# Feed-forward block of a hybrid decoder: 13 of 16 pairs of the upper projection by Strassen's scheme, lower projection by two tiles

## The chip, the cores and the metric

The kernel runs on one core of one Trainium2 chip, in one launch. The metric is the device time of that launch in microseconds (us); lower is better. The program is one long stream of instructions for five engines: TensorE (PE: matmuls and, as PEld, its weight loads), VectorE (DVE), ScalarE (ACT), GpSimd (POOL) and SyncE (SP), which here issues the DMAs. Each engine works through its own queue in order and waits at semaphores for the others.

## The reference

The reference is one inference step of a decoder layer for 512 prompt tokens and 64 sample tokens, 576 in all. After a state-space branch, an attention branch and their merge comes the part that matters here, for a residual `h` of width 1024:

```
u2 = rmsnorm(h, norm2_w)
h = h + jnp.square(jax.nn.relu(u2 @ w_up)) @ w_down     # w_up 1024x4096, w_down 4096x1024
```

and a last rmsnorm gives the outputs `y_prompt` and `y_sample`. All arrays are 32-bit floats.

## The kernel before, in words

**Precision.** TensorE reads 32-bit operands as `fp32r`, a rounded form. So each operand is kept as two tiles: `hi`, a rounded copy made by ScalarE (L122), and `lo`, the remainder raw - hi made by VectorE (L123). A product is then three matmuls, hi\*hi, hi\*lo and lo\*hi, into the same PSUM bank (`mm3`, L138 to L145). `weights` (L125 to L132) loads one 512 KB tile of weights (128 partitions x 1024) into a raw tile `wr`, of which there are two, and splits it.

**Upper projection** (L1203 to L1235). The 4096 columns of `w_up` are 32 tiles f of 128 columns. For each f and each of two halves of 288 tokens, `up` runs 8 x 3 = 24 matmuls of 128x288 (weights stationary, the tokens `u2h`, `u2l` moving) into a bank of kind `a` (three banks). ScalarE takes the relu out of the bank (L1207), VectorE squares it (L1208), ScalarE rounds it to `hh` (L1209), VectorE makes the remainder `hl` (L1211). The first three tiles are done first over 256 and then over 320 tokens (`PARTS`), so that they can start before the last tokens are normalised.

**Lower projection** (`add_product`, L1171 to L1186). Now the activations are stationary: for one of five blocks of 128 rows (four of prompt tokens; block 4 carries the hi and lo of the sample tokens side by side) and one half of the 1024 output columns, the matmuls of 128x512 over some tiles k of the inner dimension add into a bank of kind `s` (three banks). VectorE then adds that bank to the residual `h2` (L1186). Before, a group is four tiles f: 12 matmuls a bank (8 in block 4), 112 matmuls and 10 additions a group, 8 groups. The weights of a group, four row tiles of `w_down`, are split into `dh` and `dl` (seven buffers each).

**Order.** The groups are software-pipelined by hand: `ups(s + 1)` stands ahead of the lower projection of group s (L1238 to L1245). A scheduler then lays the instructions of every engine out in a fixed order, from a model of their times, before the program runs; on the chip each engine follows that order, whatever the real times are. Buffers of a tag are reused in turn, so an instruction that writes a tile can wait for the last reader of the tile that had the buffer before.

**Around it.** L1188 to L1197 are the output projection `w_out` and the second rmsnorm (`norm2`, `turn2`), which fill `u2h` and `u2l`. `final` and `last` normalise and store the result. POOL has almost nothing to do in this part.

Of the kernel before, what the change touches and what calls it, by code (L numbers as in the profile page):

```python
# [70 lines left out]
def body(ctx, tc, a, o):  # L71
# [12 lines left out]
    def pst(tag):  # L84
        return psp.tile([128, 512], FT, tag=tag, name=tag, bufs=PSB[tag])
# [22 lines left out]
    def flat(t):  # L108
        return t.rearrange("p a b -> p (a b)")
# [40 lines left out]
    def rows(src, n):  # L150
        return bass.AP(tensor=src.tensor, offset=src.offset, ap=[[0, 128], [1, n]])
# [938 lines left out]
    for t in ORDER:  # L1090
        load_x(t, h2[:, t, :])
    pool.memset(h2[64:128, 4, :], 0.0)

    p4w = ctx.enter_context(tc.tile_pool(name="p4w", bufs=1, reuse_waits="tile", side="right"))

    def row_weights(src, r0, n, at=(p4w, ("dl", "dh"), 7)):

        return [[flat(x) for x in weights([(flat, src[r0 + 128 * k:r0 + 128 * k + 128, :])], at)] for k in range(n)]

    wo = row_weights(a["w_out"][0], 0, 4)  # L1100
    def norm_rows(name):
        row = p4.tile([128, D], FT, tag="wrow", name="wrow", bufs=1)
        sy.dma_start(row, rows(a[name], D))
        return row
# [64 lines left out]
    PIECES = ((0, 512), (512, 768), (768, 1024))  # L1169

    def add_product(t, xh, xl, ws, cuts=((0, 512), (512, 1024)), banks="s"):  # L1171

        tok = slice(128 * t, 128 * t + 128)
        for c0, c1 in cuts:
            cc = slice(c0, c1)
            nb[0] += 1
            ps = pst(banks[nb[0] % len(banks)])[:, :c1 - c0]
            for k, (wh, wl) in enumerate(ws):
                if t < 4:
                    terms = (xh[k][:, tok], wh), (xl[k][:, tok], wh), (xh[k][:, tok], wl)  # L1180
                else:
                    terms = (xh[k][:, tok], wh), (xh[k][:, tok], wl)
                for i, (x, w) in enumerate(terms):
                    pe.matmul(ps, x, w[:, cc], start=(k == 0 and i == 0),  # L1184
                              stop=(k == len(ws) - 1 and i == len(terms) - 1))
            dve.tensor_tensor(h2[:, t, cc], h2[:, t, cc], ps, op=OP.add)  # L1186

    wrow = norm_rows("norm2_w")  # L1188
    turns = []
    for q in range(2):  # L1190
        ws = row_weights(a["w_out"][0], 512, 4) if q else wo
        for t in ORDER:
            add_product(t, [mgh[:, 4 * q + k, :] for k in range(4)], [mgl[:, 4 * q + k, :] for k in range(4)], ws, banks="sa")
            if q == 1:
                turns.append(norm2(t))
                if t in (0, 1, 2):
                    turns.pop(0)()  # L1197
    frow = norm_rows("final_norm_w")
    p4a_stack.close()

    p5 = ctx.enter_context(tc.tile_pool(name="p5", bufs=1, reuse_waits="tile"))

    def up(w, f, hh, hl, c0, c1):  # L1203
        ps = pst("a")
        mm3(ps, w, u2h, u2l, c0, c1)
        r = p5.tile([128, 320], FT, tag="r", name="r", bufs=3)[:, :c1 - c0]
        act.activation(r, ps[:, :c1 - c0], AF.Relu)  # L1207
        dve.tensor_tensor(r, r, r, op=OP.mult)  # L1208
        act.activation(hh[f][:, c0:c1], r, AF.Copy)  # L1209
        for dst, e0, e1 in rest(hh[f], hl[f], c0, c1):  # L1210
            dve.tensor_tensor(dst, r[:, e0 - c0:e1 - c0], hh[f][:, e0:e1].bitcast(FT), op=OP.subtract)  # L1211

    def ups(s, ws=None):
        hh = [p5.tile([128, NQ + NS], FR, tag="hh", name="hh", bufs=9) for _ in range(4)]
        hl = [p5.tile([128, NP], FR, tag="hl", name="hl", bufs=9) for _ in range(4)]

        def w_up(f):
            return whole(a["w_up"][0], 0, 512 * s + 128 * f)

        f0 = 0  # L1220
        if s == 0:
            f0 = 3
            w3 = [w_up(f) for f in range(3)]
            for c in PARTS:
                for f in range(3):
                    up(w3[f], f, hh, hl, *c)
                    if turns:
                        turns.pop(0)()
        for f in range(f0, 4):
            w = w_up(f)  # L1230
            for c in HALVES:
                up(w, f, hh, hl, *c)
            if ws is not None:
                ws += row_weights(a["w_down"][0], 512 * (s - 1) + 128 * f, 1)
        return hh, hl  # L1235

    prev = ups(0)
    for s in range(8):  # L1238
        ws = [] if s < 7 else row_weights(a["w_down"][0], 512 * s, 4)
        nxt = ups(s + 1, ws) if s < 7 else None  # L1240
        for i, t in enumerate(ORDER):
            add_product(t, *prev, ws, **({"cuts": PIECES} if s == 7 and i == 4 else {}))
            if s == 7 and i > 0:
                final(ORDER[i - 1])
        prev = nxt  # L1245
# [26 lines left out]
```

## Time and profile before

| what | value |
|---|---|
| three runs | 1486.2 us median (1485.6 to 1489.74) |
| profiled execution | 1491.02 us, span 1489.2 us |
| PE busy over the span | 1440.7 us (97%) |
| DVE busy | 975.5 us (66%) |
| ACT busy | 693.8 us (47%) |
| POOL busy | 327.7 us (22%) |
| granted TensorE clock, mean | 0.991 |

Times in the rows are us from the start of the span unless marked ns. A line such as `L145` is that of the kernel above. "busy" of a stretch is the time in which the engine had at least one instruction running; `x` counts instructions. `out<-in` gives the tiles that an instruction writes and reads; buffer numbers are left out. The span is the time between the first and the last instruction; 1.8 us of the profiled execution lie outside.

### The profile page before, as it was taken

Reading aid. Unit: us, or ns where it says so; the run is one execution under the profiler, and the core shown is the slowest. Engines: PE = TensorE matmul, PEld = TensorE weight load, DVE = VectorE, ACT = ScalarE, POOL = GpSimd, SP = SyncE. Lnnn points to the kernel's source line nnn. Section 1 sums busy time; section 2 is a strip of 40 time slices with the busy share of each in tenths; the row PEclk is TensorE's granted clock in tenths of the full one; section 3 lists DMA queues with packets and bytes.
Section 4 is the critical chain, followed back from the end, with each engine's and each line's share of the span. In section 5 each row is a group of like instructions: output and inputs, shape, how many; then the busy total and the mean of one; then the engine's idle time right before and its main releaser. Section 6 shows DMA issues by size and latency. Waiting matters only on the chain.

```text
span 1489.2 us, 26558 instructions
## 1 busy us (share of the span) xinstructions
PE 1440.7 (97%) x9964; PEld 1293.0 (87%) x9964; DVE 975.5 (66%) x2011; ACT 693.8 (47%) x1546; POOL 327.7 (22%) x479
## 2 busy tenths in 40 slices
PE   7899999999999998999999999999999999999998
PEld 6898989988887887889688888898898898899886
DVE  6699989988868667582555777665654453444435
ACT  5454365546656654443655777732352232232211
POOL 1100010426546335342323632100100000000001
PEclk9999999999999999999999999999999999999999
DMA  7324465777888877878975522146152322231202
GB/s 185 100 57 124 120 195 155 209 216 217 249 252 204 248 219 205 245 193 258 304 216 160 147 81 83 39 147 192 34 150 77 100 89 59 81 112 58 87 27 71
DMA packets 276379, 222.08 MB, mean 149 GB/s; under 512 B 39741, under 2 KB 239281, under 8 KB 276226
## 3 DMA queue, kind: packets, MB, share of 16 engines
q1 hardware_dynamic: 271002, 201.50, 47.6%
q0 software_dynamic: 5248, 18.88, 3.7%
q8 instruction: 79, 1.29, 0.4%
q14 instruction: 50, 0.41, 0.1%
HBM read 175.50 MB, written 44.07 MB: 147 GB/s over the span
## 4 chain that ended last, share of the span: by engine, by line
PE 81%; DMA 8%; DVE 5%; ACT 2%; SPq 2%; POOL 1%; issue 1%; POOLq 0%; DVEq 0%; ACTq 0%
PE w L145 25%; PE s L1184 16%; PE a L145 14%; PE w L1046 7%; PE s L1012 2%; PE a L1184 2%; PE s L878 2%; PE s L741 1%; DMA xt<-d_x 1%; PE a L1002 1%; DMA bc<-d_ac 1%; PE a L901 1%; PE s L753 1%; PE s L870 1%; DVE wl L123 1%
## 5 line engine op out<-in xcount | busy, mean ns | idle before, releaser
L145 PE MATMUL w<-uh,wh 128*128 128x288 f32 (+1 forms) x1168 | 358.4, 307 | 8.8 <-ACT tg L284 2.2
L145 PE MATMUL w<-uh,wl 128*128 128x288 f32 (+1 forms) x1168 | 354.8, 304 | 0.0
L145 PE MATMUL w<-ul,wh 128*128 128x288 f32 (+1 forms) x1168 | 352.2, 302 | 0.0
L145 PEld LDWEIGHTS w<-uh,wh 128*128 128x128 f32 x1168 | 223.4, 191 | 15.8 <-issue 3.4
L123 DVE TENSOR_TENSOR wl<-wr,wh 128x1024 fp32r<-128x1024 f32 x129 | 164.2, 1273 | 110.0 <-ACT wh L122 99.6
L145 PEld LDWEIGHTS w<-ul,wh 128*128 128x128 f32 x1168 | 223.3, 191 | 2.9 <-issue 2.2
L145 PEld LDWEIGHTS w<-uh,wl 128*128 128x128 f32 x1168 | 222.1, 190 | 1.5 <-issue 0.7
L122 ACT ACTIVATE wh<-wr 128x1024 fp32r<-128x1024 f32 x129 | 136.4, 1057 | 146.0 <-PE w L145 91.7
L145 PE MATMUL a<-u2h,wh 128*128 128x288 f32 (+2 forms) x512 | 151.4, 296 | 0.0
L145 PE MATMUL a<-u2l,wh 128*128 128x288 f32 (+2 forms) x512 | 151.2, 295 | 0.0
L145 PE MATMUL a<-u2h,wl 128*128 128x288 f32 (+2 forms) x512 | 151.2, 295 | 0.0
L122 ACT ACTIVATE dh<-wr 128x1024 fp32r<-128x1024 f32 x40 | 42.5, 1063 | 182.9 <-PE s L1184 138.3
L1186 DVE TENSOR_TENSOR h<-h,s 128x512 f32<-128x512 f32 (+1 forms) x91 | 61.1, 679 | 100.9 <-PE s L1184 100.9
L1184 PE MATMUL s<-dl,hh 128*128 128x512 f32 (+1 forms) x324 | 126.9, 392 | 0.0
L1184 PE MATMUL s<-dh,hh 128*128 128x512 f32 (+1 forms) x324 | 126.8, 392 | 0.0
L155 POOL TENSOR_TENSOR rs<-rs,cst 128x1 f32<-128x1 f32 (+2 forms) x15 | 8.3, 552 | 441.4 <-DVE rs L154 441.3
L1184 PE MATMUL s<-dh,hl 128*128 128x512 f32 (+1 forms) x260 | 101.7, 391 | 0.0
L145 PEld LDWEIGHTS a<-u2l,wh 128*128 128x128 f32 x512 | 96.1, 188 | 0.6
L145 PEld LDWEIGHTS a<-u2h,wh 128*128 128x128 f32 x512 | 96.1, 188 | 0.6
L145 PEld LDWEIGHTS a<-u2h,wl 128*128 128x128 f32 x512 | 96.1, 188 | 0.0
L123 DVE TENSOR_TENSOR dl<-wr,dh 128x1024 fp32r<-128x1024 f32 x40 | 49.0, 1225 | 49.9 <-ACT dh L122 49.8
L1046 PE MATMUL w<-ysh,wh 128*128 128x288 f32 x256 | 78.4, 308 | 0.2 <-DVE ms L1051 0.2
(390 smaller groups left out, 3220.2 us busy)
## 6 DMA issues: line engine op xcount, KB each, us to landing
wr<-in_w_in_dram SPq DMA_DIRECT2D x64, 512.0 KB
wr<-in_w_up_dram SPq DMA_DIRECT2D x32, 512.0 KB
wr<-in_w_down_dram SPq DMA_DIRECT2D x32, 512.0 KB
st<-in_state_ssm_dram SPq DMA_DIRECT2D x16, 512.0 KB
bc<-d_ac SPq DMA_DIRECT2D x32, 256.0 KB
out_dram<-st SPq DMA_DIRECT2D x16, 512.0 KB
wr<-in_w_ssm_proj_dram SPq DMA_DIRECT2D x16, 512.0 KB
EB<-d_ec SPq DMA_DIRECT2D x40, 128.0 KB
```

The costliest lines, as they stand in the source:

```text
L122: act.activation(hi, raw, AF.Copy)
L123: (lo_eng or dve).tensor_tensor(lo, raw, hi.bitcast(FT), op=OP.subtract)
L145: pe.matmul(ps[:, :c1 - c0], p[:, k, :], x[:, c0:c1], start=(k == 0 and i == 0), stop=(k == 7 and i == 2))
L741: pe.matmul(py[64 * (hh % 2):64 * (hh % 2) + 64, 128 * (hh // 2):128 * (hh // 2) + n], xt[:n, 64 * hh:64 * hh + 64], mt, start=True, stop= ...
L753: pe.matmul(pi[:, 128 * i:128 * i + 128], G.hT[:, 128 * i:128 * i + 128], CT[:, c0:c0 + n], start=True, stop=True)
L870: pe.transpose(pv[:, i, :], Kg[q][:, 256 * i + 128 * hp:256 * i + 128 * hp + 128], idf)
L878: pe.matmul(v[64 * hp:64 * hp + 64], QZ[:, hp, :], kk, start=True, stop=True)
L901: pe.matmul(py[h, 0:128], PTs[:, s, h], Vg[s // 4][:, 256 * (s % 4) + 128 * hp:256 * (s % 4) + 128 * hp + 128], start=(s == 0), stop=False)
L1012: pe.matmul(py[64 * e:64 * e + 64, 0:256], Vt[:, j, kv:kv + 64], PT[:, e, j], start=(j == 0), stop=False)
L1046: pe.matmul(ps[:, :HQ], p[:, k, mc], x[k][:, c0:c1], start=(k == 0 and i == 0), stop=(k == 3 and i == 2))
L1184: pe.matmul(ps, x, w[:, cc], start=(k == 0 and i == 0), stop=(k == len(ws) - 1 and i == len(terms) - 1))
L1186: dve.tensor_tensor(h2[:, t, cc], h2[:, t, cc], ps, op=OP.add)
```

## The change

The 32 column tiles of `w_up` are taken as 16 pairs. Six tiles (three pairs) are computed as before. The other 13 pairs are computed by a scheme of the Strassen-Winograd kind: the pair's 1024x256 weights are four blocks of 512x128 (a11, a12 in the raw tile `left`, a21, a22 in `right`; the inner dimension is cut in two, and the two tiles f are the other index), the tokens are four blocks of 512x288. Seven block products of 4 x 3 = 12 matmuls take the place of eight. The sums of weights are made in place in the raw tiles by VectorE (four subtractions or additions of 128x512 a pair), and the four forms that arise are split: `fa` and `fb` into the usual buffers `wh`/`wl` (three of each), `fc` into `gh`/`gl` and `fd` into `eh`/`el`, of which there is one each. The raw tiles of every other pair come from a second pair of buffers, `wr2`. The sums of token blocks are made once, in `token_sums`; one of them overwrites a block of `u2h`, `u2l`. Products are combined on VectorE (`plus`, seven a pair, one operand in PSUM), then squared. The squaring moves from VectorE to ScalarE. Halves of tokens are laid out as 256 prompt tokens and 32 sample tokens each.

The lower projection runs by groups of two tiles f in place of four (14 groups, and one of four at the end), with four buffers each for `dh`, `dl` in a new pool that takes the place of the pool of `w_out`; the latter has six buffers in place of seven.

```diff
-    def row_weights(src, r0, n, at=(p4w, ("dl", "dh"), 7)):
+    WO = (p4w, ("dl", "dh"), 6)
+    wo = row_weights(a["w_out"][0], 0, 4, WO)
...
+    def squared(src, x, h, r=None):
+        hh, hl = x
+        r = small("r", 3) if r is None else r
+        act.activation(r, src, AF.Relu)
+        act.activation(r, r, AF.Square)
+        p, q = slice(256 * h, 256 * h + 256), slice(NP + 32 * h, NP + 32 * h + 32)
+        act.activation(hh[:, p], r[:, 0:256], AF.Copy)
+        act.activation(hh[:, q], r[:, 256:HQ], AF.Copy)
+        dve.tensor_tensor(hl[:, p], r[:, 0:256], hh[:, p].bitcast(FT), op=OP.subtract)
+        dve.tensor_tensor(hh[:, NQ + 32 * h:NQ + 32 * h + 32], r[:, 256:HQ], hh[:, q].bitcast(FT), op=OP.subtract)
...
+    def token_sums():
+        E = (dve, dve, dve, dve)
+        for k in (0, 2):
+            def B(i, j):
+                return [u[:, 4 * i + k:4 * i + k + 2, HQ * j:HQ * j + HQ].bitcast(FT) for u in (u2h, u2l)]
+            v, w = [flat(q5.tile([128, 8, 128], FT, tag="wr2", name="tr", bufs=2))[:, 0:2 * HQ].rearrange("p (k c) -> p k c", k=2)
+                    for _ in range(2)]
...
+            diff(v, b12, b11, E[0])
+            done(th[:, 0, k:k + 2], tl[:, 0, k:k + 2], v)
+            less(v, b22, v, E[2])
+            done(th[:, 1, k:k + 2], tl[:, 1, k:k + 2], v)
+            less(w, b21, v, E[3])
+            done(th[:, 2, k:k + 2], tl[:, 2, k:k + 2], w)
+            diff(v, b22, b12, E[1])
+            done(u2h[:, k:k + 2, HQ:NQ], u2l[:, k:k + 2, HQ:NQ], v)
+
+    tags = ["a", "w", "a", "a", "w"]
+
+    def quick_pair(f):
+        hh = act_tiles(2)
+        at = (q5, "wr2") if f % 4 else (wp, "wr")
+        left, right = [at[0].tile([128, 8, 128], FT, tag=at[1], name=at[1], bufs=2) for _ in range(2)]
+        for i, x in enumerate((left, right)):
+            sy.dma_start(x, block(w_up, 0, 128 * f + 128 * i))
+        a11, a12, a21, a22 = left[:, 0:4], left[:, 4:8], right[:, 0:4], right[:, 4:8]
...
+        fa = two(wp, ("wh", "wl"), WB[1])
+        split(left, *fa)
+        fd = two(p5, ("eh", "el"), 1, 4)
+        split(a22, *fd)
+        dve.tensor_tensor(a22, a21, a22, op=OP.add)
+        dve.tensor_tensor(a21, a11, a21, op=OP.subtract)
+        dve.tensor_tensor(a11, a22, a11, op=OP.subtract)
+        dve.tensor_tensor(a12, a12, a11, op=OP.subtract)
+        fb = two(wp, ("wh", "wl"), WB[1])
+        fc = two(p5, ("gh", "gl"), 1)
+        for (h_, l_), x in ((fb, right), (fc, left)):
+            split(x, h_, l_)
...
+        p1 = small("p1", 1)
+        act.copy(p1, product(fa, 0, B(0, 0)))
+        s2 = plus("s2", product(fc, 0, T(1)), p1)
+        c = plus("r", product(fa, 1, B(1, 0)), p1)
+        squared(c, hh[0], 0, c)
+        s3 = plus("s3", product(fb, 0, T(2)), s2)
+        p5_ = product(fb, 1, T(0))
+        c = plus("r", p5_, s3)
+        squared(c, hh[1], 1, c)
+        s2 = plus("s2", p5_, s2)
+        c = plus("r", product(fd, 0, T(3)), s3)
+        squared(c, hh[1], 0, c)
+        c = plus("r", product(fc, 1, B(1, 1)), s2)
+        squared(c, hh[0], 1, c)
+        return hh
...
+    blocks = [hh[0:2], hh[2:4]] + [plain_pair(2 * p) for p in range(2, FIRST)]
+    token_sums()
+    for s in range(14):
+        ws = row_weights(w_down, 256 * s, 2, WD)
+        p = s + 2
+        if p >= FIRST:
+            blocks.append(quick_pair(2 * p))
         for t in ORDER:
+            add_product(t, [stationary(x, t) for x in blocks[s]], ws)
...
+    ws = row_weights(w_down, 256 * 14, 2, WD) + row_weights(w_down, 256 * 15, 2, (wp, ("wh", "wl"), WB[1]))
```

Here `FIRST` is 3, `diff(x, p, q)` is three VectorE instructions of 128x576, `less` two, `done` a rounded copy on ScalarE and a subtraction on VectorE; `hh` and `hl` have six buffers in place of nine.

## Rows read from the trace of the kernel before

**Rows 1.** The page's head and engine line: busy us, share of the span, instructions.
```profile
span 1489.2 us, 26558 instructions
PE 1440.7 (97%) x9964; PEld 1293.0 (87%) x9964; DVE 975.5 (66%) x2011; ACT 693.8 (47%) x1546; POOL 327.7 (22%) x479
```

**Rows 2.** Windows: stretch, PE, PEld, DVE, ACT, POOL busy, PEclk, DMA share, GB/s.
```profile
1073.99:1479.11 405.12, 405.12 (x2375) 364.69 (x2374) 185.88 (x310) 115.55 (x196) 2.20 (x4) 1.00 0.27 81
...
1222.82:1274.53 51.71, 51.71 (x305) 46.59 (x305) 23.06 (x39) 14.37 (x24) 0.00 (x0) 1.00 0.28 83
```

**Rows 3.** The chain that ended last: start, us, engine, bank, line, instructions.
```profile
1073.99 45.41 PE a L145 x336
...
1222.82 6.52 PE s L1184 x28
1229.34 0.80 PE a L145 x6
1230.13 19.59 PE s L1184 x84
1249.72 24.80 PE a L145 x186
```

**Rows 4.** Timeline of VectorE in one group: start, us, line, operation.
```profile
1226.41 0.45 DVE L1208 TENSOR_TENSOR r<-r 128x288 f32<-128x288 f32 x1
1226.79 0.68 DVE L1186 TENSOR_TENSOR h<-h,s 128x512 f32<-128x512 f32 x1
1227.38 1.22 DVE L123 TENSOR_TENSOR dl<-wr,dh 128x1024 fp32r<-128x1024 f32 x1
1228.52 0.38 DVE L1211 TENSOR_TENSOR hl<-r,hh 128x224 fp32r<-128x224 f32 x1
1228.82 0.22 DVE L1211 TENSOR_TENSOR hh<-r,hh 128x64 fp32r<-128x64 f32 x1
1228.96 1.27 DVE L1186 TENSOR_TENSOR h<-h,s 128x512 f32<-128x512 f32 x2
```

**Rows 5.** Groups by line and shape: busy us, mean ns, idle before, releaser.
```profile
L1186 DVE TENSOR_TENSOR h<-h,s 128x512 f32<-128x512 f32 x79 | 53.6, 686 | 99.0 <-PE s L1184 98.9
...
L122 ACT ACTIVATE dh<-wr 128x1024 fp32r<-128x1024 f32 x32 | 34.0, 1063 | 172.1 <-PE s L1184 138.3 <-DMA wr<-in_w_down_dram 33.6
...
L1209 ACT ACTIVATE hh<-r 128x288 fp32r<-128x288 f32 x58 | 25.3, 442 | 41.0 <-DVE r L1208 40.7
L1207 ACT ACTIVATE r<-a 128x288 f32<-128x288 f32 x58 | 22.6, 399 | 28.7 <-PE a L145 28.7
...
L1211 DVE TENSOR_TENSOR hl<-r,hh 128x256 fp32r<-128x256 f32 x6 | 2.5, 422 | 1.5 <-ACT hh L1209 1.5
```

**Rows 6.** VectorE groups of the whole span: a sum with one operand in PSUM.
```profile
L1051 DVE TENSOR_TENSOR ms<-ms,w 128x288 f32<-128x288 f32 x48 | 21.5, 450 | 13.0 <-PE w L1046 12.8
```

**Rows 7.** Windows in the input projection, where VectorE is loaded most.
```profile
150.00:200.00 50.00, 48.73 (x361) 48.01 (x360) 45.65 (x75) 20.17 (x47) 3.72 (x10) 1.00 0.53 147
200.00:250.00 50.00, 48.08 (x358) 47.48 (x357) 45.47 (x60) 29.80 (x69) 7.00 (x20) 1.00 0.59 168
250.00:300.00 50.00, 48.54 (x385) 47.10 (x385) 48.47 (x60) 27.36 (x63) 16.05 (x24) 1.00 0.69 198
450.00:500.00 50.00, 47.57 (x356) 41.65 (x356) 41.01 (x79) 32.41 (x80) 32.25 (x37) 1.00 0.81 219
```

**Rows 8.** Timeline of the DMA queue: the issue of one load of weights.
```profile
1264.58 0.33 SPq L130 DMA_DIRECT2D wr<-in_w_down_dram  x1
```

**Rows 9.** Timeline of ScalarE: the first use of that load, and its wait.
```profile
1269.30 1.06 ACT L122 ACTIVATE dh<-wr 128x1024 fp32r<-128x1024 f32 x1 [2.49 <-DMA wr<-in_w_down_dram]
```

More of the change, by code (lines that the diff above doesn't have):

```diff
@@ L1092, in body @@
     pool.memset(h2[64:128, 4, :], 0.0)
-    p4w = ctx.enter_context(tc.tile_pool(name="p4w", bufs=1, reuse_waits="tile", side="right"))
-    def row_weights(src, r0, n, at=(p4w, ("dl", "dh"), 7)):
[L1098 to L1104, printed above, removed]
     ssq = p4.tile([128, 12], FT, name="ssq2")
@@ L1109, in body, with row_weights, less_rounded, row_weights_by_dma @@
     u2l = p4.tile([128, 8, NQ], FR, name="u2l")
-    def row_norm(t, i):
+    p4w_stack = ctx.enter_context(ExitStack())
+    pn = p4w_stack.enter_context(tc.tile_pool(name="pn", bufs=1, reuse_waits="tile", side="right"))
+    p4w = p4w_stack.enter_context(tc.tile_pool(name="p4w", bufs=1, reuse_waits="tile", side="right"))
+    def row_weights(src, r0, n, at):
+        return [[flat(x) for x in weights([(flat, src[r0 + 128 * k:r0 + 128 * k + 128, :])], at)] for k in range(n)]
+    def less_rounded(lo, hi, src):
+        act.activation(lo, hi.bitcast(FT), AF.Copy, scale=-1.0)
+        pool.dma_start(out=lo, in_=src, accum_op=OP.add)
+    def row_weights_by_dma(src, r0, n, at):
+        out = []
+        for k in range(n):
+            lo, hi = [flat(at[0].tile([128, 8, 128], FR, tag=x, name=x, bufs=at[2])) for x in at[1]]
+            rows_ = src[r0 + 128 * k:r0 + 128 * k + 128, :]
+            pool.dma_start(out=hi, in_=rows_)
+            less_rounded(lo, hi, rows_)
+            out.append([hi, lo])
+        return out
+    WO = (p4w, ("dl", "dh"), 6)
+    wo = row_weights(a["w_out"][0], 0, 4, WO)
+    def jrow():
+        return pn.tile([128, D], FT, tag="jk", name="jk", bufs=2)
+    def row_norm(t, i, row):
         n = 128 if t < 4 else 64
@@ L1115, in row_norm @@
         if t == 4:
-            other = p4.tile([128, D], FT, tag="jk", name="other", bufs=2)[:64]
+            other = row()[:64]
             sy.dma_start(other, h2[64:128, 4, :])
             dve.tensor_tensor(src, src, other, op=OP.add)
-        jk = p4.tile([128, D], FT, tag="jk", name="jk", bufs=2)[:n]
-        act.activation(jk, src, AF.Square, accum_out=ssq[:n, i:i + 1])
+        act.activation(row()[:n], src, AF.Square, accum_out=ssq[:n, i:i + 1])
         rstd_of(rs[:n, i:i + 1], ssq[:n, i:i + 1], D, 1, n)
@@ L1142, in turn2 @@
                 pe.transpose(pv[:, i, :], xn[:, 128 * k:128 * k + 128], idf[:n, :n])
-            h_ = u2h[:, m * q:m * q + m, 128 * t:128 * t + n]
-            act.activation(h_, pv, AF.Copy)
-            dve.tensor_tensor(u2l[:, m * q:m * q + m, 128 * t:128 * t + n], pv, h_.bitcast(FT), op=OP.subtract)
+            if t < 4:
+                c = HQ * (t // 2) + 128 * (t % 2)
+                h_, l_ = [u[:, m * q:m * q + m, c:c + 128] for u in (u2h, u2l)]
+            else:
+                h_, l_ = [u.rearrange("p k (h c) -> p k h c", h=2)[:, :, :, 256:HQ] for u in (u2h, u2l)]
+                pv = pv.rearrange("p k (h c) -> p k h c", h=2)
@@ new lines, in turn2, with add_product @@
+            act.activation(h_, pv, AF.Copy)
+            dve.tensor_tensor(l_, pv, h_.bitcast(FT), op=OP.subtract)
+    PIECES = ((0, 512), (512, 768), (768, 1024))
+    def add_product(t, xs, ws, cuts=((0, 512), (512, 1024)), banks="s"):
+        for c0, c1 in cuts:
+            cc = slice(c0, c1)
+            nb[0] += 1
+            ps = pst(banks[nb[0] % len(banks)])[:, :c1 - c0]
+            for k, (wh, wl) in enumerate(ws):
+                x = xs[k]
+                terms = [(x[0], wh), (x[1], wh), (x[0], wl)] if t < 4 else [(x[0], wh), (x[0], wl)]
+                for i, (p, w) in enumerate(terms):
+                    pe.matmul(ps, p, w[:, cc], start=(k == 0 and i == 0),
+                              stop=(k == len(ws) - 1 and i == len(terms) - 1))
+            dve.tensor_tensor(h2[:, t, cc], h2[:, t, cc], ps, op=OP.add)
@@ new lines, in body @@
+    wrow = pn.tile([128, D], FT, name="wrow")
+    sy.dma_start(wrow, rows(a["norm2_w"], D))
+    turns = []
+    for q in range(2):
+        ws = row_weights(a["w_out"][0], 512, 4, WO) if q else wo
+        for t in ORDER:
+            tok = slice(128 * t, 128 * t + 128)
+            add_product(t, [[mgh[:, k, tok]] + ([mgl[:, k, tok]] if t < 4 else []) for k in range(4 * q, 4 * q + 4)], ws, banks="sa")
+            if q == 1:
+                turns.append(norm2(t))
+                if t in (0, 1, 2):
+                    turns.pop(0)()
@@ new lines, in body, with act_tiles, small @@
+    p4a_stack.close()
+    FIRST = 3
+    p5 = ctx.enter_context(tc.tile_pool(name="p5", bufs=1, reuse_waits="tile"))
+    w_up, w_down = a["w_up"][0], a["w_down"][0]
+    def act_tiles(n):
+        return [(p5.tile([128, NQ + NS], FR, tag="hh", name="hh", bufs=6), p5.tile([128, NP], FR, tag="hl", name="hl", bufs=6))
+                for _ in range(n)]
+    def small(tag, bufs):
+        return p5.tile([128, HQ], FT, tag=tag, name=tag, bufs=bufs)
+    def squared(src, x, h, r=None):
[8 more added lines that the diff above has]
+        dve.tensor_tensor(hh[:, NQ + 32 * h:NQ + 32 * h + 32], r[:, 256:HQ], hh[:, q].bitcast(FT), op=OP.subtract)
@@ new lines, in stationary, with up, plain_pair @@
+    def stationary(x, t):
+        hh, hl = x
+        return [hh[:, 128 * t:128 * t + 128], hl[:, 128 * t:128 * t + 128]] if t < 4 else [hh[:, NP:NQ + NS]]
+    def up(w, hh, h):
+        ps = pst("a")
+        mm3(ps, w, u2h, u2l, HQ * h, HQ * h + HQ)
+        squared(ps[:, :HQ], hh, h)
+    def plain_pair(f):
+        hh = act_tiles(2)
+        for i in range(2):
+            w = whole(w_up, 0, 128 * (f + i))
+            for h in range(2):
+                up(w, hh[i], h)
+        return hh
@@ new lines, in body, with two, product, B @@
+    tags = ["a", "w", "a", "a", "w"]
+    def quick_pair(f):
+        hh = act_tiles(2)
+        at = (q5, "wr2") if f % 4 else (wp, "wr")
[3 more added lines that the diff above has]
+        a11, a12, a21, a22 = left[:, 0:4], left[:, 4:8], right[:, 0:4], right[:, 4:8]
+        def two(pool_, names, bufs, k=8):
+            return [pool_.tile([128, k, 128], FR, tag=n, name=n, bufs=bufs) for n in names]
+        fa = two(wp, ("wh", "wl"), WB[1])
[10 more added lines that the diff above has]
+            split(x, h_, l_)
+        def product(form, i, xs):
+            tags.append(tags.pop(0))
+            ps = pst(tags[-1])[:, :HQ]
+            w = [q[:, 4 * i:4 * i + 4] for q in form]
+            for k in range(4):
+                for j, (p, q) in enumerate(((w[0], xs[0]), (w[0], xs[1]), (w[1], xs[0]))):
+                    pe.matmul(ps, p[:, k, :], q[:, k, :], start=(k == 0 and j == 0), stop=(k == 3 and j == 2))
+            return ps
+        def B(i, j):
+            return [u[:, 4 * i:4 * i + 4, HQ * j:HQ * j + HQ] for u in (u2h, u2l)]
+        def T(i):
+            return [u[:, 0:4, HQ:NQ] for u in (u2h, u2l)] if i == 2 else [x[:, min(i, 2)] for x in (th, tl)]
+        def plus(tag, ps, q):
+            d = small(tag, 3 if tag == "r" else 2)
+            dve.tensor_tensor(d, ps, q, op=OP.add)
+            return d
+        p1 = small("p1", 1)
[12 more added lines that the diff above has]
+        squared(c, hh[0], 1, c)
+        return hh
@@ L1167, in last @@
             sy.dma_start(o[0][0, 128 * t:128 * t + 128, cc], y[:, cc])
[L1169 to L1191, printed above, removed]
-        for t in ORDER:
[L1193 to L1245, printed above, removed]
+    hh = act_tiles(4)
+    w3 = [whole(w_up, 0, 128 * f) for f in range(3)]
+    for h in range(2):
+        for f in range(3):
+            up(w3[f], hh[f], h)
+            if turns:
+                turns.pop(0)()
@@ new lines, in body @@
+    w = whole(w_up, 0, 384)
+    for h in range(2):
+        up(w, hh[3], h)
+    p4w_stack.close()
+    q5 = ctx.enter_context(tc.tile_pool(name="q5", bufs=1, reuse_waits="tile", side="right"))
+    WD = (q5, ("dl", "dh"), 4)
+    th = q5.tile([128, 3, 4, HQ], FR, tag="th", name="th")
+    tl = q5.tile([128, 3, 4, HQ], FR, tag="tl", name="tl")
+    blocks = [hh[0:2], hh[2:4]] + [plain_pair(2 * p) for p in range(2, FIRST)]
+    token_sums()
+    fin = None
+    for s in range(14):
[3 more added lines that the diff above has]
+            blocks.append(quick_pair(2 * p))
+        for t in ORDER:
+            add_product(t, [stationary(x, t) for x in blocks[s]], ws)
@@ new lines, in body, with frows @@
+    fin = [q5.tile([128, 3, 4, HQ], FT, tag=n, name="fin", bufs=1).rearrange("p a b c -> p (a b c)") for n in ("th", "tl")]
+    slots = [f[:, D * i:D * i + D] for f in fin for i in range(3)]
+    frow = slots.pop(0)
+    sy.dma_start(frow, rows(a["final_norm_w"], D))
+    def frows():
+        slots.append(slots.pop(0))
+        return slots[-1]
+    ws = row_weights(w_down, 256 * 14, 2, WD) + row_weights(w_down, 256 * 15, 2, (wp, ("wh", "wl"), WB[1]))
+    for i, t in enumerate(ORDER):
+        add_product(t, [stationary(x, t) for s in (14, 15) for x in blocks[s]], ws, **({"cuts": PIECES} if i == 4 else {}))
+        if i > 0:
+            final(ORDER[i - 1])
```

19 lines of the change are left out of this document (15 added, 4 removed).

## The prediction

> **What bounds the kernel now.** First the page's engine line: PE is busy 97% of the span, VectorE 66%, ScalarE 47% [rows 1]. Then the stretch from the last transposes of the second rmsnorm to the last lower product, in the windows: PE is busy 405.12 of 405.12 us at a granted clock of 1.00, VectorE 185.88 us, ScalarE 115.55 us, and the DMA engines carry 27% [rows 2]. So this stage is bound by TensorE and by nothing else; the other engines have slack, VectorE more than half. Third the chain of waits, which in this stage is PE alone, in a pattern that repeats every 51.7 us [rows 3]: 28 + 84 = 112 lower matmuls in 6.52 + 19.59 = 26.11 us, that is 0.233 us each, and 6 + 186 = 192 upper ones in 25.60 us, that is 0.1333 us each. The mean of a matmul's own row would be longer, since neighbours overlap; what counts is this pace.
>
> **What the change takes off TensorE.** A pair of tiles f costs 2 x 2 x 24 = 96 matmuls of 128x288 as it stands and 7 x 12 = 84 by the scheme. The shape is the same, so 12 x 0.1333 = 1.60 us a pair, and 13 pairs give 20.8 us. The lower matmuls stay 896 of the same shape, so nothing is gained or lost there. One new step (one pair, one group of two tiles) takes 84 x 0.1333 + 56 x 0.233 = 11.20 + 13.06 = 24.26 us of PE, where two tiles take 51.71 / 2 = 25.86 us now.
>
> **What it puts on VectorE.** The timeline shows starts of neighbouring instructions [rows 4]: one of 1024 elements holds the queue 1.14 us (1227.38 to 1228.52), one of 512 0.59 us, of 288 0.38 us, of 224 0.30 us, of 64 0.14 us; from these I estimate 0.34 us for 256 and 0.11 us for 32. A step then has:
> - two remainders of `w_down`, 2 x 1.14 = 2.28 us (as before for two tiles);
> - weights of the pair: three remainders of 1024 and one of 512, and four sums of 512: 3.42 + 0.59 + 2.36 = 6.37 us. An addition of two SBUF tiles is not in the trace at 512; at 288 SBUF operands and a PSUM operand cost the same (0.45 us each, [rows 4, 6]), so I take the 0.59;
> - seven `plus`, 7 x 0.38 = 2.66 us, and four times the remainders of 256 and of 32, 1.80 us; the squares are gone to ScalarE;
> - ten additions to the residual in place of five, 5.90 us. This is the price of groups of two tiles.
>
> Sum 19.0 us of a step of 24.26 us, 78%. From the other side, with the whole duration of each row (0.686, 1.22, 0.450, 0.422 us, [rows 4 to 6], and estimates of 0.69 for a sum of 512 and 0.19 for 32) it is 22.0 us, 91%. Before, it is 23.06 / 2 = 11.5 us of 25.86 us [rows 2]. So VectorE nearly doubles its work and stays below PE on either count.
>
> The rows overlap: the remainder that begins at 1227.38 lasts 1.22 us, and the next begins 0.08 us before it ends [rows 4]. The Trainium skill (VectorE: DVE Perf Modes, The DRAIN you can't avoid) says that the next operation does not start until the pipe is empty, and its rules for authors ask for few operations above all; by that the 22.0 us would be the right sum, by the rows the 19.0, and neither reaches 24.26.
>
> **ScalarE.** Rows of 1.06 us for 1024 and 0.40 us for 288 [rows 5]: five roundings of 1024 and one of 512 (estimate 0.6), one copy, and four times relu, square, copy of 256 and of 32 (estimate 0.40 + 0.40 + 0.42 + 0.19) make 5.3 + 0.6 + 0.4 + 5.6 = 11.9 us a step, half of it. No bound; moving the square there costs nothing while this holds.
>
> **DMA.** A step loads 2 MB as two tiles did; before, 27% of the engines are used. One load of 512 KB beside another takes 4.7 us from issue to use [rows 8, 9]. A pair's raw tiles are now held through the sums, but every other pair has buffers of its own; I cost this at nothing, covered by the 13 us of lower matmuls; uncovered, it would be those 4.7 us a pair.
>
> **Where PE can wait.** `fc` and `fd` have one set of buffers. The next pair's `fd` can be written when product 6 of this pair has been read, and the chain from there to `fc` ready is: rounding 0.6, remainder 0.59, four sums 2.36, rounding 1.06, two remainders 2.28, together 6.9 us. It has time until product 2 of the next pair: product 7 (1.6), the lower group (13.06), product 1 (1.6), that is 16.3 us. On VectorE's queue the ten additions (5.9), the `w_down` remainders (2.28) and the last combinations (about 1.6) stand among it; all in a row that is 16.7 us. This is tight, but the `w_down` remainders have two steps of buffers and can go elsewhere, and the order can run a lower group ahead, since pairs are made two groups early. A lower bank now fills in 6 x 0.233 = 1.4 us where it took 2.8, and there are three, so a late addition has 2.8 us before PE stops. How much PE loses I bound by rows: nothing, as in this stage now with VectorE busy 45% [rows 2], or the 4.65 us of 150 (3.1%) that PE is idle between 150 and 300 with VectorE busy 93% [rows 7]. Of 13 x 24.26 = 315 us that is 0 to 9.8 us. VectorE at 78 to 91% is nearer the loaded row, but most of what waits there are other things than weights; I take 4 us.
>
> **The start.** Token sums are 2 x 14 instructions of 576 elements, 0.66 us each by the same pace, 18.5 us of VectorE. From 1074 PE has 240 plain matmuls left, 32 us, to about 1106. The last sum overwrites tokens that the plain pairs read, so it ends behind them, and its work tiles are the `wr2` in which the first pair's weights must land. I count about 6 us for the sums left over, 6 us for two loads and 9 us for the weights, so `fc` is ready near 1127 or, beside the additions, 1132. PE has the groups 0, 1 and 2 of 13.06 us to fill that, to 1145. So it is hidden, if the order takes them first; I put 2 us for it, for the sixth buffer of `w_out` and for the last pair. Between nothing and 10 us; all of it if only group 0 lies there.
>
> **Sum.** -20.8 + 4 + 2 = -14.8 us. From the profiled 1491.0 us that gives 1476.2; the median of the runs is 4.8 us below the profiled execution, so 1471.4 us.
>
> **The rivals.**
> - *VectorE eats most of it.* With PE short by 4.9%, as in 450 to 500 with VectorE busy 82% [rows 7], 14 steps of 24.26 us lose 16.5 us: 1486.2 - 20.8 + 16.5 = 1482 us, about no change. For it: the same load on VectorE. Against: POOL is busy 32 of 50 us there and idle here.
> - *The start is not hidden.* The order puts the first pair ahead of groups 1 and 2; PE waits 8 to 10 us: 1486.2 - 20.8 + 4 + 10 = 1479 us.
> - *The weight chain is exposed, and it is slower.* VectorE works in order, and its additions wait for PE (98.9 us before 79 of them, [rows 5]). If the planned order puts the last two remainders of the chain behind the lower group's last addition, product 2 waits for 2.28 us in each pair: 13 x 2.28 = 29.6 us, and 1486.2 - 20.8 + 29.6 = 1495 us. It decides from 1.6 us a pair on. For it: single buffers, and 16.7 us of work for 16.3 us of time. Against: the order is laid out with such waits in view, and there is no wait of PE in this stage now.
>
> **How the numbers follow.** The likeliest, 1465 to 1478 with 1471.4 in it: 0.54. Start not hidden, 1479: 0.12. VectorE eats it, 1482: 0.15. Chain exposed, 1495: 0.19. A measurement of this kernel tells about 0.3% (4.5 us) from no change, so below 1481.7 counts as faster: the first two and a little of the third, 0.70; same 0.13; slower 0.17. The range 1464 to 1488 holds the first three.
>
> **What would show it.** In the windows after: upper and lower matmuls at 0.1333 and 0.233 us, VectorE 78 to 91% busy in the stage, ScalarE near half. PE's idle time before `fc`'s products (the chain or the start) or before lower products (late additions) would be in the list of waits; over 20 us in all refutes the forecast, as would matmuls of another pace.

## The result, and the profile after

The changed kernel runs in 1467.6 us (median of 4, 1462.62 to 1471.29) against 1485.9 us before in the same series (1482.59 to 1489.74): ratio 0.9874, 95% interval 0.9836 to 0.9912, so 18 us faster. The forecast was 1471.4 us, 1464 to 1488, faster at 0.70.

First the page's engine line of the changed kernel, which answers to [rows 1]:

```profile
span 1460.8 us, 26653 instructions
PE 1421.3 (97%) x9808; PEld 1273.8 (87%) x9808; DVE 1100.5 (75%) x2246; ACT 757.2 (52%) x1721; POOL 328.8 (23%) x479
```

156 matmuls fewer (13 x 12), and VectorE busy for 125 us more. The span is 28.4 us shorter than that of before, which is more than the medians say. Where the rest is from shows in when the first matmul of `w_out` starts: up to there TensorE's instructions are the same in both kernels. The rows are from the view of that line, before and after (duration min/median/max in ns, first and last start):

```profile
L1184 PE MATMUL a<-dh,mgh x40: 389/395/479, 998.8 to 1065.7; 128*128 128x512 f32 x40
```

```profile
L1181 PE MATMUL a<-dh,mgh x40: 390/396/732, 988.3 to 1058.5; 128*128 128x512 f32 x40
```

In these two executions the unchanged front part differs by 10.5 us; over the thirteen profiles of this document, all with the same 7160 matmuls up to there, it takes from 986.2 to 998.8 us, so that difference says nothing of the change. From the first `w_out` matmul to the end of the span it is 1489.2 - 998.8 = 490.4 us before and 1460.8 - 988.3 = 472.5 us after, 17.9 us less, which agrees with the medians. I call this stretch the tail; all profiles below are compared by it. (The expectations say 490.2 for before, counted from the chain's piece that starts 0.2 us later.)

The chain of waits after, around the feed-forward stage, beside [rows 3] (start, us, engine, bank, line, instructions; L1306 are the matmuls of the scheme, L1181 the lower ones):

```profile
1067.48 32.00 PE a L145 x240
1099.48 10.27 PE s L1181 x44
...
1123.20 2.12 PE a L1306 x16
1125.32 1.39 PE s L1181 x6
...
1235.23 0.94 PE a L1306 x7
...
1240.67 1.60 PE w L1306 x12
...
1415.14 35.55 PE s L1181 x152
```

The paces are 32.00 / 240 = 0.1333 us, 1.60 / 12 = 0.133 us and 10.27 / 44 = 0.233 us, as before. Lower matmuls no longer come in blocks of 112; the scheduler that fixes the order (the planner, below) threads groups of six between the products. The last piece ends at 1450.69. From the mark of the last transposes to there it is 1450.69 - 1067.48 = 383.2 us, where it was 1479.11 - 1073.99 = 405.1 us.

The windows, beside [rows 2] (stretch, PE, PEld, DVE, ACT, POOL busy, PEclk, DMA share, GB/s):

```profile
990.00:1067.48 77.48, 75.76 (x402) 64.90 (x401) 43.47 (x69) 22.81 (x37) 4.68 (x7) 0.98 0.36 108
...
1099.48:1145.00 45.52, 45.52 (x249) 39.79 (x249) 42.36 (x70) 21.25 (x39) 0.00 (x0) 1.00 0.36 105
```

```profile
1145.00:1415.00 270.00, 270.00 (x1578) 242.66 (x1577) 216.54 (x391) 124.19 (x260) 0.00 (x0) 1.00 0.29 85
```

In the steady part PE is busy 270 of 270 us with VectorE at 80% and ScalarE at 46%; in the 45 us ahead of it VectorE is at 93%. The one place where PE stops lies ahead of the stage, in the `w_out` stretch, where busy time falls 1.72 us short and the clock to 0.98.

### The profile page after: what moved, and what is told of

Same layout as the page of the kernel before. It is cut to its first block, busy times and chain, and to the rows that moved or that the text cites. A ratio compares the mean times of both kernels' runs of the same rounds, so it can differ in the third digit from the quotient of the medians.

```text
span 1460.8 us, 26653 instructions
## 1 busy us (share of the span) xinstructions
PE 1421.3 (97%) x9808; PEld 1273.8 (87%) x9808; DVE 1100.5 (75%) x2246; ACT 757.2 (52%) x1721; POOL 328.8 (23%) x479
## 4 chain that ended last, share of the span: by engine, by line
PE 81%; DVE 7%; DMA 6%; SPq 2%; ACT 2%; issue 2%; POOL 1%; DVEq 0%; POOLq 0%; ACTq 0%
PE w L145 27%; PE s L1181 15%; PE w L1046 7%; PE a L1306 6%; PE w L1306 4%; PE a L145 3%; PE s L1012 2%; PE s L878 2%; PE a L1181 1%; DMA wr<-in_w_ssm_proj_dram 1%; PE s L741 1%; PE a L1002 1%; PE a L901 1%; DMA bc<-d_ac 1%; PE s L753 1%
## 5 line engine op out<-in xcount | busy, mean ns | idle before, releaser
L123 DVE TENSOR_TENSOR wl<-wr,wh 128x1024 fp32r<-128x1024 f32 x129 | 160.0, 1241 | 74.9 <-ACT wh L122 73.8
L1183 DVE TENSOR_TENSOR h<-h,s 128x512 f32<-128x512 f32 (+1 forms) x161 | 108.5, 680 | 58.5 <-PE s L1181 58.2
L1181 PE MATMUL s<-dh,hh 128*128 128x512 f32 (+1 forms) x302 | 119.1, 394 | 0.0
L1181 PE MATMUL s<-dl,hh 128*128 128x512 f32 (+1 forms) x302 | 118.8, 393 | 0.0
L1181 PE MATMUL s<-dh,hl 128*128 128x512 f32 (+1 forms) x242 | 95.0, 393 | 0.0
L1046 PE MATMUL w<-ysh,wl 128*128 128x288 f32 x256 | 76.8, 300 | 0.0
L1046 PE MATMUL w<-ysl,wh 128*128 128x288 f32 x256 | 76.7, 300 | 0.0
L728 ACT ACTIVATE bc<-bc,acum 128x128 f32<-128x128 f32 (+1 forms) x160 | 48.5, 379 | 41.9 <-DMA bc<-d_ac 41.7
L590 DVE SCALAR_TENSOR_TENSOR ca<-rb,cwT,ca 128x616 f32<-128x616 f32 x72 | 68.8, 957 | 0.3
L1181 PEld LDWEIGHTS s<-dl,hh 128*128 128x128 f32 x302 | 56.7, 188 | 12.5
L1181 PEld LDWEIGHTS s<-dh,hh 128*128 128x128 f32 x302 | 56.7, 188 | 10.2 <-DVE h L1183 0.5
L740 DVE SCALAR_TENSOR_TENSOR bc<-bc,dts,cb 128x128 f32<-128x128 f32 (+1 forms) x160 | 56.9, 419 | 0.3
```

What stands on the lines that cost most here:

```text
L590: dve.scalar_tensor_tensor(ca[:, 0:616], rb[:, k:k + 616], cwT[:, 24 * k + ct:24 * k + ct + 1], ca[:, 0:616], op0=OP.mult, op1=OP.add)
L728: act.activation(bc[:n, i, :n], bc[:n, i, :n], AF.Relu, scale=-1.0, bias=acum[:n, c, h0 + i:h0 + i + 1])
L740: dve.scalar_tensor_tensor(mt, mt, dts[:n, c, 8 * g + hh:8 * g + hh + 1], cb[:n, :n], op0=OP.mult, op1=OP.mult)
L1046: pe.matmul(ps[:, :HQ], p[:, k, mc], x[k][:, c0:c1], start=(k == 0 and i == 0), stop=(k == 3 and i == 2))
L1181: pe.matmul(ps, p, w[:, cc], start=(k == 0 and i == 0), stop=(k == len(ws) - 1 and i == len(terms) - 1))
```

## The experiments

All are timed beside runs of the kernel before on the same chip. The tail is read from one profile of each kernel. It is split at the first upper matmul behind the last transposes of the second rmsnorm: the `w_out` stretch is what lies ahead of it, the stage goes from it to the end of the last matmul (both from the timelines of PE). What is left is 7.3 us in every kernel but E7. Where two kernels have the same instructions in a stretch, it repeats closely: 79.0 to 79.1 us of `w_out` stretch in the changed kernel, E8 and E10, 75.7 in E3 and E9. The changed layout puts 0.7 us of upper matmuls more into the `w_out` stretch and takes them out of the stage (48 matmuls of 288 tokens in place of 256).

| run | ratio to before, interval | tail, us | `w_out` stretch | stage |
|---|---|---|---|---|
| before | 1 | 490.4 | 74.9 | 408.2 |
| changed | 0.9874 (0.9836 to 0.9912) | 472.5 | 79.0 | 386.3 |
| E1 no pair by the scheme | 1.0021 (0.9998 to 1.0044) | 492.3 | 77.1 | 407.9 |
| E2 seven pairs | 0.9924 (0.9897 to 0.9951) | 480.5 | 76.9 | 396.3 |
| E3 changed, seven `w_out` buffers | 0.9841 (0.9812 to 0.9870) | 469.1 | 75.7 | 386.1 |
| E4 before, six `w_out` buffers | 1.0005 (0.9985 to 1.0024) | 493.8 | 78.3 | 408.2 |
| E5 four sums more a pair | 0.9921 (0.9888 to 0.9953) | 481.0 | 78.1 | 395.6 |
| E6 eight | 0.9926 (0.9896 to 0.9956) | 480.4 | 77.7 | 395.4 |
| E7 twelve | 1.0040 (1.0012 to 1.0069) | 495.1 | 76.8 | 395.3 |
| E8 one set of raw buffers | 0.9872 (0.9818 to 0.9926) | 474.5 | 79.1 | 388.2 |
| E9 14 pairs, seven buffers | 0.9885 (0.9855 to 0.9915) | 475.5 | 75.7 | 392.5 |
| E10 chain longer by four | 0.9850 (0.9809 to 0.9891) | 472.4 | 79.1 | 386.0 |
| E11 chain longer by eight | 0.9996 (0.9971 to 1.0021) | 489.8 | 77.4 | 405.0 |

### E1 and E2: the pairs alone

```diff
-            blocks.append(quick_pair(2 * p))
+            blocks.append(plain_pair(2 * p))                                   # E1, and no token_sums()
+            blocks.append(quick_pair(2 * p) if p % 2 == 1 else plain_pair(2 * p))   # E2
```

In E2 the plain pairs read the token block that the sums have overwritten; their instructions and shapes are the same, but the outputs are no longer those of the reference.

> All 16 pairs plain, token sums left out; the two-tile lower groups, the layout and the six w_out buffers stay. Theory (TensorE counts alone; VectorE's ten additions per two tiles are hidden): from the first w_out matmul to the end 490.2 us of before, plus about 4 us of the w_out stretch, less 1.1 us for the equal halves: 493 us, so the run is about 3 us above before. Rival (groups of two tiles cost PE time at the three banks): more than 8 us above before.

> Seven pairs by the scheme (every other one), six plain. Theory: 1.60 us for each of them, so 7 x 1.60 = 11.2 us below the kernel with all pairs plain, and 6 x 1.60 = 9.6 us above the changed kernel (472.4 us from the first w_out matmul to the end), 482 us. Rival (the pairs lose part of it where VectorE is crowded): with alternate pairs VectorE has more room, so less than 9.6 us above the changed kernel, or even no difference.

E1's tail is 492.3 us, 1.9 above before and 1.5 below E4, which has its six buffers in the old scheme. Its stage, with the 0.7 us that moved, is 408.6 us against 408.2. So the groups of two tiles, with ten additions per two tiles on VectorE, cost TensorE about 0.4 us.

By the tails E2 is 11.8 us below E1 (11.2 expected), and the changed kernel 8.0 us below E2 (9.6 expected), which looks like a loss where every pair is by the scheme. The stages show that it is none: E1 to E2 11.6 us for seven pairs, E2 to the changed kernel 10.0 us for six, together 21.6 us, 1.66 us a pair where 1.60 was counted. The difference lies in the `w_out` stretch, 79.0 us in the changed kernel and 77 in E1 and E2; the next section has its cause. So the gain goes by the number of matmuls, and VectorE takes no part of it. Why a pair gives 0.06 us more than counted stays open.

### E3 and E4: the sixth buffer of `w_out`

```diff
-    WO = (p4w, ("dl", "dh"), 6)
+    WO = (p4w, ("dl", "dh"), 7)        # E3; E4 puts 6 for 7 in the kernel before
```

> The changed kernel with seven w_out buffers as before. Theory (the sixth buffer delays the second rmsnorm; PE stops 1.7 us for its transposes and then runs at half clock for some 3.4 us): PE's stop near the transposes goes, and from the first w_out matmul to the end it is 472.4 - 4.0 = 468.4 us. Rival (the token layout or the planner's other order is the cause): within 1 us of 472.4.

> The kernel before with six w_out buffers in place of seven, nothing else. Theory: the w_out stretch gets 4 us longer, 490.2 + 4 = 494 us from the first w_out matmul to the end. Rival (it takes the rest of the change): within 1 us of 490.2.

E3 takes 3.4 us off the tail, E4 adds 3.4 us to it: the same price in both kernels, and all of it in the `w_out` stretch, so the buffer is the cause and the token layout is not. (The price is that of the profiles. The medians do not resolve it: E4's interval holds 1, and those of E3 and the changed kernel overlap.) The way it costs shows in the chain of the changed kernel (start, us, what):

```profile
1021.75 2.80 PE a L1181 x12
...
1025.10 1.07 ACT dh L122
...
1027.34 1.23 DVE dl L123
...
1028.59 4.95 DMA wr<-in_w_up_dram
...
1033.56 1.07 ACT wh L122
...
1035.80 1.29 DVE h L1183 x2
...
1037.14 5.71 DMA jk<-h
...
1042.94 1.23 DVE h L1136
...
1048.89 1.30 DVE jk L1147
...
1050.23 0.65 PE a L1159 x4
...
1051.38 4.29 PE a L1181 x12
```

Two tiles of weights instead of one wait for their buffers at 1025. The raw tiles come free later, so a load of `w_up` starts later; its remainder stands in VectorE's queue ahead of the additions to the residual, the additions release the DMA that the sample tokens' norm needs, and TensorE waits for the normalised rows. The wait itself, in the timeline of PE, is 1.72 us; behind it the rows are 0.43 us apart, where the same matmul takes 0.233 us:

```profile
1050.23 0.65 PE L1159 MATMUL a<-cst,jk 128*128 128x128 f32 x4 [1.72 <-DVE jk L1147]
...
1052.03 0.63 PE L1181 MATMUL a<-dl,mgh 128*128 128x512 f32 x1
1052.46 0.63 PE L1181 MATMUL a<-dh,mgh 128*128 128x512 f32 x1
```

```profile
1052.00:1054.00 2.00, 2.00 (x6) 1.60 (x5) 1.93 (x4) 0.01 (x1) 0.55 (x1) 0.50 0.00 0
```

The granted clock of that window is 0.50, the lower of its two levels (1.2 GHz): 12 matmuls take 4.29 us instead of 2.80. So here a short wait cost nearly as much again in clock. In E3's tail the list of waits of PE is empty.

The wait is in the profiles of all ten kernels with six buffers, 0.97 to 1.98 us long, and in none of the three with seven (before, E3, E9). The fall of the clock does not always follow. It came behind the waits of 1.72 us (changed), 1.78 (E8), 1.80 (E4) and 1.83 (E10), and not behind those of E1, E2, E7 and E11 (0.97 to 1.61) nor behind the longest two, 1.89 us in E6 and 1.98 in E5. There, at the same place, the rows are 0.23 us apart and the clock is 1.00 (a row of PE and a window of E5):

```profile
1057.04 0.66 PE L1159 MATMUL a<-cst,jk 128*128 128x128 f32 x4 [1.98 <-DVE jk L1147]
```

```profile
1057.00:1062.00 5.00, 4.96 (x29) 4.12 (x30) 4.92 (x8) 1.55 (x3) 0.55 (x1) 1.00 0.00 0
```

What decides between the two these runs do not show. The sixth buffer costs about 3.3 us where the clock falls and 1.1 to 2.4 us where it does not (the `w_out` stretch against E3's 75.7).

### E5 to E7: more work on VectorE

```diff
+        for _ in range(4):             # 8 in E6, 12 in E7; at the end of quick_pair
+            dve.tensor_tensor(extra.rearrange("p (a b) -> p a b", a=2), u2h[:, 4:6, 0:256].bitcast(FT), u2l[:, 4:6, 0:256].bitcast(FT), op=OP.add)
```

> The changed kernel with four more VectorE sums of 128x512 in each of the 13 pairs, written to a tile that nothing reads. By the pace of neighbouring rows (0.59 us each) VectorE has 19.0 + 2.4 = 21.4 us of a step of 24.26 us: no change, within 2 us of 472.5 us from the first w_out matmul to the end. Rival (whole durations count, the pipe empties between operations): 22.0 + 4 x 0.686 = 24.7 us, VectorE is the bound, 13 x 0.5 = 6 us longer.

> Eight more sums a pair. By the pace of neighbouring rows 19.0 + 4.7 = 23.7 us of 24.26: at the edge, 0 to 10 us longer than 472.5. Rival (whole durations): 27.5 us a step, 13 x 3.2 = 42 us longer.

> Twelve more sums a pair. By the pace of neighbouring rows 19.0 + 7.1 = 26.1 us a step, VectorE is the bound: 13 x 1.8 = 24 us longer than 472.5, a little less for what the ends of the stage can take. Rival (whole durations): 30.2 us a step, 13 x 6 = 78 us longer.

Four and eight sums cost the same, 8.5 and 7.9 us, and not where either theory put it: since nothing orders these sums, the planner filled VectorE's queue with them early, 45 to 47 of them ahead of 1200 in E5, E6 and E7 alike. In the windows of E6, before and from 1200 on:

```profile
1066.00:1200.00 134.00, 127.72 (x767) 113.56 (x766) 129.56 (x221) 62.77 (x128) 0.55 (x1) 1.00 0.29 87
```

```profile
1200.00:1400.00 200.00, 200.00 (x1166) 179.47 (x1165) 191.32 (x352) 93.81 (x202) 0.00 (x0) 1.00 0.29 85
```

At the start, where VectorE has little room (93% in the changed kernel), PE is idle for 6.3 us of 134; the longest entry in its list of waits there is for the additions to the residual, which free the lower banks:

```profile
PE s L1181 <- DVE h L1183: 3.6, 5, 0.9
```

Idle time understates the loss: rows of PE overlap (lower ones last 0.39 us and start 0.233 us apart), so a delay shorter than the overlap leaves no gap. The stage is 9.1 us longer than in the changed kernel, the tail only 7.9, because the clock did not fall in E6's `w_out` stretch. Later PE is busy 200 of 200 us beside a VectorE at 96%, and the matmuls of that window, at 0.1333 and 0.233 us each, are 200 us of work: nothing is lost. VectorE's share is much the same in both windows, 97% and 96%, so it is not the share that costs the time early, but (argued, not shown) what the added sums stand in front of there: token sums, first weights and additions. And the 352 VectorE instructions of that window, each count times its mean duration, sum to 219.9 us in 200 us: their durations overlap, and the pace of neighbouring rows is the right price. The expected 42 us of the other count did not come; the measured 8 us lie within my range, by another place than expected.

E7's tail is 22.6 us longer than that of the changed kernel, near the 24 that I expected, but not for that reason: its stage is that of E5 and E6. The 14.7 us on top of E6 are sums that were left over and run at the very end, behind the last normalisation, with nothing else to do:

```profile
1468.03 15.93 DVE L1336 TENSOR_TENSOR extra<-u2h,u2l 128x512 f32<-128x512 f32 x22
```

So no run here shows what a VectorE that is too slow throughout would cost.

### E8: the second set of raw buffers

```diff
-        at = (q5, "wr2") if f % 4 else (wp, "wr")
+        at = (wp, "wr")
```

> The changed kernel with the raw weights of every pair in the two buffers that w_down uses too, so without the second set. Theory (transfers are hidden behind 13 us of lower products): within 2 us of 472.5. Rival (the second set is what hides them): up to 4.7 us of a load exposed in every second pair, 6 x 4.7 = 28 us longer, so slower than before.

2.0 us longer, 1.9 of them in the stage, so the second set is worth about 2 us. The waits of PE that show there are 1.3 us for additions to the residual; none is for a load or for weights. Loads stay hidden with one set, and how it costs the 2 us was not followed.

### E9: one pair more

```diff
-    FIRST = 3
+    FIRST = 2                          # and seven buffers as in E3
```

> Seven w_out buffers and 14 pairs by the scheme (two plain pairs ahead in place of three). Theory (TensorE counts): one pair more takes 1.6 us off, 469.1 - 1.6 = 467.5 us from the first w_out matmul to the end. Rival (the start is where VectorE has no room, as 52 to 104 added sums cost 8 us there): 12.8 us less plain work covers the token sums, PE waits some us for the first pair, so 469 to 478.

The tail is 475.5 us, 6.4 above E3 in place of 1.6 below: the rival. The chain leaves PE at the start (start, us, what):

```profile
1109.15 0.75 DVE tr L1263
...
1114.61 4.12 DMA wr<-in_w_up_dram
...
1119.84 1.23 DVE wl L123
...
1122.36 4.33 DMA wr<-in_w_up_dram
...
1134.29 4.53 PE w L1306 x20
```

Token sums, then loads into the tiles that these sums had used, then the weights: the path that I laid out for the start. It is not the first pair that waits. With two plain pairs the first pair by the scheme has another parity and takes the ordinary raw tiles (its `fd` is rounded at 1085.27); the second one takes `wr2`, which the sums hold. Its remainder `el` stands in VectorE's queue ahead of the `plus` that frees a bank, and PE waits for that:

```profile
1126.72 0.63 ACT L122 ACTIVATE eh<-wr 128x512 fp32r<-128x512 f32 x1 [2.37 <-DMA wr<-in_w_up_dram]
1127.38 0.69 DVE L123 TENSOR_TENSOR el<-wr,eh 128x512 fp32r<-128x512 f32 x1 [1.35 <-ACT eh L122]
1129.83 0.40 PE L1306 MATMUL w<-u2h,wh 128*128 128x288 f32 x1 [2.46 <-DVE s L1318]
```

Behind the wait the clock falls here too, to its lower level:

```profile
1131.20:1137.80 6.60, 6.08 (x22) 5.03 (x22) 6.60 (x14) 5.72 (x14) 0.00 (x0) 0.50 0.28 79
```

So of the 8.0 us between forecast and tail about 4 are idle time of PE and, by an estimate from these 6.6 us at half the clock, some 3 are the clock. Three plain pairs cover the path, two do not.

### E10 and E11: a longer weight chain

```diff
+        for _ in range(4 if f >= 10 else 0):    # 8 in E11; behind the four sums of weights
+            dve.tensor_tensor(a12, a12, a12, op=OP.max)
```

> The changed kernel with four more VectorE operations of 128x512 inside the weight chain of each of the last 11 pairs (behind the four sums, ahead of the remainders, on the same tile, values unchanged): the chain grows from 6.9 to 9.3 us, the step from 19.0 to 21.4 us of VectorE. Theory (pairs are made far enough ahead, and lower products fill PE): within 2 us of 472.5 from the first w_out matmul to the end. Rival (the chain through the single buffers has no slack): 11 x 2.4 = 26 us longer.

> Eight such operations: the chain 11.6 us, VectorE 23.7 us of a step of 24.26. Theory: 0 to 6 us longer than 472.5, since VectorE's pace still fits. Rival (single buffers): 11 x (11.6 - 6.9) = 52 us longer, less at most 16.3 - 6.9 us of slack once.

Four operations cost nothing (472.4 against 472.5 us), eight cost 17.3 us. By their own pace they are 2.4 and 4.7 us a pair, but the chain grows by far more, because the planner puts other rows between two of them in VectorE's queue. From the remainder of `fd` (`el`) to the end of the remainder of `fc` (`gl`) one pair takes 11.0 us in the changed kernel, 18.2 in E10 and 31.8 in E11 (rows of VectorE, in this order):

```profile
1389.45 0.68 DVE L123 TENSOR_TENSOR el<-wr,eh 128x512 fp32r<-128x512 f32 x1
...
1399.25 1.22 DVE L123 TENSOR_TENSOR gl<-wr,gh 128x1024 fp32r<-128x1024 f32 x1
```

```profile
1275.37 0.68 DVE L123 TENSOR_TENSOR el<-wr,eh 128x512 fp32r<-128x512 f32 x1
...
1292.30 1.22 DVE L123 TENSOR_TENSOR gl<-wr,gh 128x1024 fp32r<-128x1024 f32 x1
```

```profile
1340.15 0.69 DVE L123 TENSOR_TENSOR el<-wr,eh 128x512 fp32r<-128x512 f32 x1 [0.29 <-ACT eh L122]
...
1370.76 1.21 DVE L123 TENSOR_TENSOR gl<-wr,gh 128x1024 fp32r<-128x1024 f32 x1
```

The medians over the last eleven pairs are 11.0, 18.7 and 33.2 us, and 20.5 in E6, which lost nothing late in the stage. So the chain has slack up to some 20 us, and at 33 us it has none. The list of waits of E11 has `fc` first (who waited for whom: us, times, longest):

```profile
PE a L1308 <- ACT gh L122: 3.5, 1, 3.5
PE s L1181 <- ACT hh L1218: 2.2, 1, 2.2
PE s L1181 <- DVE dl L123: 1.3, 1, 1.3
```

Only part of the 17.3 us is that wait. In the stage PE is idle for 10.2 us, of which 3.7 wait for `gh`; the rest are mostly lower products that wait for `hh`, for weights of `w_down` or for additions, rows that stand in the same queues. Behind two of the stops the clock falls:

```profile
1314.00:1320.80 6.80, 6.37 (x14) 4.58 (x15) 5.60 (x10) 1.06 (x1) 0.00 (x0) 0.50 0.54 148
1443.80:1447.00 3.20, 3.00 (x12) 3.00 (x13) 1.23 (x1) 0.15 (x1) 0.00 (x0) 0.50 0.00 0
```

VectorE was not full there:

```profile
1060.00:1476.00 416.00, 405.84 (x2317) 358.52 (x2316) 368.98 (x650) 184.57 (x384) 3.93 (x7) 0.99 0.27 80
```

That is 89%, less than in E6's quiet window. E11 lies between my theory (0 to 6 us) and the rival (52 us less its slack): the theory was wrong in that VectorE's share alone decides. One thing is not separated: the planner lays out a new order for each of these kernels, so E11 differs from the changed kernel in its order too.

## Why the prediction was right

**TensorE's saving, -20.8 us.** Right: from the mark to the last lower matmul of the chain 21.9 us less, of which 0.7 is only moved across the mark (48 upper matmuls ahead of it are 5.66 us before, of 256 tokens, and 6.38 us after, of 288); the stages of E1 and the changed kernel give 21.6.

**Loss in the steady part, +4 us of 0 to 9.8.** Mis-sized: it is 0 (270 of 270 us). The loaded windows of [rows 7], from which the upper end came, did not carry over: with VectorE at 96% late in E6 PE lost nothing. So VectorE's share alone does not make such a loss. E11 shows one thing that does, a chain that a product waits for; whether that is what cost PE its time in the input projection no run here shows.

**Where PE can wait.** The 6.9 us counted for the weight chain were too few. Without its first rounding they are 6.3 us, and the rows show 11.0, because other rows of VectorE stand between those of the chain. It did no harm, since the slack was larger than the chain: E10's 18.7 us were still free.

**VectorE and ScalarE.** The count by the pace of neighbouring rows was 78% and by whole durations 91%; measured 80%. The rows of the new operations are as taken from their nearest ones: `plus` 0.45 us, a sum of 512 0.69 us (0.60 apart). ScalarE 46%, forecast near half. The Trainium skill says that the next operation waits until the pipe is empty, and at the same place that one which is not held starts earlier (VectorE: DVE Perf Modes, The DRAIN you can't avoid). As a price the first does not hold here, and the trace agrees with the second: 219.9 us of durations ran in 200 us (E6).

**The start.** Right in the mechanism. `fc` of the first pair was ready at 1126.9, 59.4 us behind the mark, where I had 53 to 58. PE filled it with 1.7 lower groups and other products. E9, E5 and E6 show that little more fits there.

**The buffer of `w_out`.** Named, but within 2 us together with the start; it is 3.3 us of the `w_out` stretch (3.4 in E3's and E4's tails), 1.7 of them the wait and most of the rest the clock. I had not followed what is queued behind the later load: VectorE's additions, a DMA, the norm, and then the clock. So the sum came to -17.9 us by -21.2 (stage, less the 0.7) + 0 + 3.3, where I had -20.8 + 4 + 2 = -14.8: two terms off in opposite ways. The mechanism was right; that the sum came within 4 us was in part luck.

**The rivals.** Chain exposed: not in this kernel, but real with eight operations more a pair (E11), not with four (E10). VectorE eats most: no. Start not hidden: no with three plain pairs, yes with two (E9).

The best version is E3: 1464.7 us (median of 6, 1460.64 to 1468.51), 0.9841 of before; its tail is 21.3 us below that of before and 3.4 below that of the changed kernel; the intervals of the two ratios overlap.

## What to carry to other kernels

Where TensorE is the bound and VectorE half idle, matmuls can be bought with sums; price VectorE by the distance between starts of neighbouring rows, not by their durations. What decided here was not its share but the longest chain that a product waits for, measured with all that stands between its rows in the queue, and the room at the start, where one-time sums meet the first weights. Read a small loss stretch by stretch: by the tails alone VectorE seemed to take 1 us of the gain, and it took none. When a pool loses a buffer, follow the later load through every queue that stands behind it to the engine that is the bound.

## What was not expected

VectorE at 96% busy beside a TensorE without a gap for 200 us (E6). And the price of a short wait: 1.72 us of idle PE were followed by a granted clock of 0.50 that made 12 matmuls 1.5 us longer, while behind 1.98 us at the same place in E5 the clock stayed at 1.00. And four added operations of 0.60 us each made a chain 7.7 us longer, at no cost.
